# A hybrid convolution block on one core: constants on ScalarE's DMA queue, first-half squares later, the last A tile scaled by VectorE and used last in four output tiles

## The chip, the core and the metric

The kernel runs on one core of a Trainium2 chip. Five engines work side by side, each through its own instructions in order: TensorE (PE; its weight loads are listed as PEld), VectorE (DVE), ScalarE (ACT), GpSimd (POOL) and SyncE (SP). They wait for each other through semaphores. Transfers between the chip's main memory (HBM) and the on-chip memory (SBUF) are issued from the queues of SP, ACT or POOL and run on 16 DMA engines. Matmul results land in PSUM banks of 128 x 512 float32. The metric is the device time of one execution in microseconds (us); lower is better.

## The reference, cut to what matters

```python
h = rmsnorm(x, norm_mix_g)                       # x: 1024 positions x 1024 channels
z = h @ w_in                                     # 1024 -> 2560 columns
a_h, a_bg, a_cg, b_val, b_gate = split(z)        # 512 columns each
y_a = a_bg * dwconv(a_cg * a_h, conv_a_w)        # 3 taps
u = b_val * sigmoid(b_gate)
u = dwconv(u, conv_b_w) + conv_b_b               # 31 taps
y_b = silu(layernorm(u, ln_b_g, ln_b_b))
x = x + concat(y_a, y_b) @ w_out                 # 1024 -> 1024
h = rmsnorm(x, norm_ffn_g)
g = dwconv(h @ w_gate, conv_ffn_w)               # 1024 -> 2816
v = h @ w_up
x = x + (silu(g) * v) @ w_down
return rmsnorm(x, norm_final_g)
```

## The kernel before

Activations lie transposed: channels on the 128 partitions, the 1024 positions along the row, worked on as two halves h = 0 and 1 of 512. A channel tile is 128 channels, so a contraction over 1024 channels is eight steps k. To keep float32 accuracy every operand is split into a rounded part hi and a remainder lo, and each product is three matmuls: hi by hi, hi by lo, lo by hi (lines 152 to 154 are those three in the output stage, line 166 in the input projection, line 271 in its first two tiles).

**Start (lines 248 to 282).** The transfers of x go on SP's queue in pieces (line 249 on), the first two weight tiles `win01` on ACT's queue in three pieces of 2, 2 and 4 steps k (`load_w01`, `cuts`), and the constants `cst` (gains, conv taps, biases; 119 KB) on POOL's queue (line 251). For each half and each k, `load_h1` makes hi (ACT, line 213) and lo (DVE, line 214) of x times its gain, which needs `cst`; `split_w01` makes hi (a cast) and lo (a subtraction) of the weights on DVE; then six matmuls follow (three for each of the weight tiles `pg` and `pv`). `sq_h1` squares x on ACT (lines 221, 224) and adds the square to `acc1[h]` (line 226), on POOL for the whole first half and for k = 1, 2 of the second, else on DVE. `stat_h1` turns the sum into 1/rms: the sum over partitions is two matmuls with a tile of ones (`total_parts`, `total_of`, lines 179 to 186), then a root on ACT and a reciprocal on DVE (lines 193, 194). The first half's stands behind k = 3 of the second half, the second half's behind step k = 5 of the next weight tile. Since 1/rms is applied to the products, the matmuls don't wait for it, but the B tiles do.

**B tiles and conv (lines 288 to 343).** Four B tiles u are made from pairs of products; the 31-tap convolution over them is done mostly by DVE, a tap an instruction (line 315), into `cv` in PSUM and at last into `c`. It is put behind everything urgent by a priority offset.

**A tiles (lines 346 to 367).** Four tiles j: m = c times h times 1/rms squared, the three taps into y (ACT line 359, DVE lines 360 and 361), y times 1/rms (`r1`, on POOL, line 362), times b from PSUM (DVE, line 366), and the split into `yA` (hi on ACT, lo on POOL).

**Layernorm and output projection (lines 370 to 468).** `layernorm(h)` makes the four B tiles `yB[h]` from `c`: sums on DVE, totals on PE, the division (line 385), silu and hi on ACT, lo on DVE. The contraction of the output projection runs over yA tiles 0 to 3 (k = 0 to 3) and yB tiles 0 to 3 (k = 4 to 7). For the first half, the first HEAD = 4 output tiles dt are begun with the A tiles 0 to 2 (`range(NJ - 1)`) and finished, after `layernorm(0)`, with A tile 3 and the B tiles. Then come the other four tiles of the first half and eight of the second; `out_done` adds x and sums squares.

The rest is the feed-forward part (two-level products with seven instead of eight block products, line 546) and the final norm; its code isn't touched. Most of the program is put in order by a scheduler that estimates the times of instructions itself and takes `urgent` (raised priority) and `late` into account; only where a `manual_schedule` names an engine does that engine keep the written order. PE has it in the start.

Of the kernel before, what the change touches and what calls it, by code (L numbers as in the profile page):

```python
# [45 lines left out]
def block_kernel(ctx: ExitStack, tc, xT, win01, win, wout, wgate, wup, wdown, consts, outT):  # L46
# [196 lines left out]
    def split_w01(a, b):  # L243
        for i, (hi, lo) in enumerate(w01):
            nc.vector.tensor_copy(hi[:, a:b, :], raw01[:, a:b, i, :])
            minus(nc.vector, lo[:, a:b, :], raw01[:, a:b, i, :], f32(hi[:, a:b, :]))

    cuts = ((0, 2), (2, 4), (4, 8))
    nc.sync.dma_start(xs[0][:, 0, :], xT[0, :, 0])
    load_w01(*cuts[0])  # L250
    nc.gpsimd.dma_start(cst, consts)
    nc.sync.dma_start(xs[0][:, 1, :], xT[0, :, 1])
# [8 lines left out]
    with tc.manual_schedule(engines={nc.tensor.engine}):  # L261
        for h in range(2):
            for k in range(KD):
                load_h1(h, k)
                if h == 0:
                    for a, b in cuts:
                        if k == a:
                            split_w01(a, b)
                for wz, xz in ((0, 0), (0, 1), (1, 0)):
                    for pt, w in zip((pg, pv), w01):  # L270
                        nc.tensor.matmul(pt[h], w[wz][:, k, :], a1(h, k)[xz], start=k + wz + xz == 0, stop=k == KD - 1 and wz == 1)  # L271
                sq_h1(h, k)
                if h == 1 and k == 3:
                    with urgent():
                        stat_h1(0)

        def late_stat(k):
            if k == 5:
                with urgent():
                    stat_h1(1)  # L280
# [65 lines left out]
    for j in range(NJ):  # L346
# [8 lines left out]
        with urgent():  # L355
# [5 lines left out]
            nc.vector.scalar_tensor_tensor(y[:, : S - 1], m[:, 1:], col(W_A + 3 * j + 2), y[:, : S - 1], ALU.mult, ALU.add)  # L361
            pool(y, y, r1, ALU.mult)
        pb = mm_tile(base + 2, a1)
# [29 lines left out]

    def out_mm(pt, e, w, h, ks):
        for k in ks:
            mm3(half(pt, e), w[0][:, k, :], w[1][:, k, :], *y_of(h, k), k == 0, k == KD - 1)

# [44 lines left out]
    for h in range(2):  # L442
# [8 lines left out]
        for dt in range(head):  # L451
            start(dt)
            out_mm(pts[dt // 2], dt % 2, ws[dt], h, range(NJ - 1))
        if h == 0:
# [3 lines left out]
        for dt in range(KD):  # L458
            nc.sync.dma_start(half(xr[dt], h), xT[h, :, dt])
            if dt >= head:  # L460
                start(dt)
            out_mm(pts[dt // 2], dt % 2, ws[dt], h, range(NJ - 1 if dt < head else 0, KD))
            out_done(pts[dt // 2], dt, h, accs2[h])
# [683 lines left out]
```

## Time and profile before

| | |
|---|---|
| times of three runs | 1007.45, 1007.51, 1008.87 us; median 1007.51 |
| profiled execution | 1008.48 us, its span 1006.7 us |
| busy in the span | PE 967.7 us (96%), DVE 744.7 (74%), ACT 447.2 (44%), POOL 441.3 (44%) |
| chain that ended last | PE 85%, DVE 7%, issue 3%, DMA 2%, ACT 2%, POOL 1% |

The span is the profiled part of an execution. PE is busy nearly throughout, so the time is PE's work plus the places where PE stands idle or runs at the lower clock. A view of waits says what PE waited for; a timeline by engine shows the instructions of a stretch with their durations and, in brackets, the idle time ahead and who ended it. Neighbouring instructions of one form are merged (x2, x7), and a duration includes the overlap with the next instruction.

### The profile page before, as it was taken

The page shows a single profiled execution, that of the slowest core. Times are in us where ns is not written, and L with a number is a line of the kernel's source. Part 1 is how long each engine was busy: PE and PEld are TensorE (multiplying, and loading weights), DVE is VectorE, ACT ScalarE, POOL GpSimd, SP SyncE. Part 2 cuts the span into 40 slices and gives each one's busy share as a digit, 9 for nine tenths or more (in the row PEclk, how much of TensorE's full clock was granted, in tenths as well). Part 3 has the DMA queues.
Part 4 walks back from the last instruction along what each step waited for, and adds up shares of the span by engine and source line. Part 5 has one row for each costly group of instructions (what it writes and reads, how often), then busy time and mean ns, then how long its engine had stood idle before and what let it go on. Part 6 is the DMA issues. An engine that isn't in the chain of part 4 may idle for free.

```text
span 1006.7 us, 11592 instructions
## 1 busy us (share of the span) xinstructions
PE 967.7 (96%) x4208; PEld 792.3 (79%) x4208; DVE 744.7 (74%) x893; ACT 447.2 (44%) x626; POOL 441.3 (44%) x301
## 2 busy tenths in 40 slices
PE   5999999998999999899999999999999899999994
PEld 4888888886888887788888888888777688888883
DVE  7899999999679797754654554564559798796556
ACT  7354421234564446443443443443447253543353
POOL 4189853344763005454344345335324545352006
PEclk9999999999999999999999999999999999999998
DMA  6211111123564203233223232223375753643205
GB/s 255 84 43 63 42 43 63 42 63 105 177 210 129 91 1 120 100 105 132 78 105 121 89 105 108 102 94 106 109 241 172 236 163 109 195 135 101 68 0 168
DMA packets 63178, 112.56 MB, mean 112 GB/s; under 512 B 5488, under 2 KB 26992, under 8 KB 62864
## 3 DMA queue, kind: packets, MB, share of 16 engines
q1 hardware_dynamic: 62640, 110.65, 33.1%
q10 hardware_dynamic: 432, 1.05, 0.3%
q8 instruction: 33, 0.54, 0.2%
q14 instruction: 25, 0.20, 0.1%
q0 software_dynamic: 48, 0.12, 0.0%
HBM read 84.79 MB, written 27.00 MB: 111 GB/s over the span
## 4 chain that ended last, share of the span: by engine, by line
PE 85%; DVE 7%; issue 3%; DMA 2%; ACT 2%; POOL 1%; SPq 0%; POOLq 0%; DVEq 0%; ACTq 0%
PE a L546 28%; PE mm L166 19%; PE c L546 13%; PE b L546 7%; PE mm L152 3%; PE mm L154 3%; PE mm L153 3%; PE a L681 2%; PE mm L271 2%; PE c L681 1%; DVE r L93 1%; DVE wlo L93 1%; PE y L154 1%; PE y L152 1%; PE y L153 1%
## 5 line engine op out<-in xcount | busy, mean ns | idle before, releaser
L166 PE MATMUL mm<-r,whi 128*128 128x512 f32 x576 | 155.3, 389 | 0.0
L546 PE MATMUL a<-r,whi 128*128 128x512 f32 x472 | 147.4, 393 | 5.6 <-ACT a L531 4.6
L315 DVE SCALAR_TENSOR_TENSOR cv<-u,cst,cv 128x512 f32<-128x512 f32 x203 | 138.9, 748 | 0.7
L166 PEld LDWEIGHTS mm<-r,whi 128*128 128x128 f32 x576 | 108.1, 188 | 22.5
L546 PE MATMUL c<-r,whi 128*128 128x512 f32 x392 | 120.7, 389 | 0.0
L93 POOL TENSOR_TENSOR wlo<-raw,whi 128x1024 fp32r<-128x1024 f32 x30 | 76.7, 2556 | 83.0 <-ACT whi L131 83.0
L131 ACT ACTIVATE whi<-raw 128x1024 fp32r<-128x1024 f32 (+1 forms) x68 | 69.3, 1020 | 97.1 <-PE mm L166 33.0
L546 PEld LDWEIGHTS a<-r,whi 128*128 128x128 f32 x472 | 89.1, 189 | 26.4 <-ACT a L531 5.5
L500 POOL TENSOR_TENSOR s<-up 128x512 f32<-128x512 f32 (+1 forms) x31 | 43.2, 1395 | 135.5 <-DMA up<-wup 118.8
L500 POOL TENSOR_TENSOR s<-raw,s 128x512 f32<-128x512 f32 (+1 forms) x31 | 40.1, 1292 | 138.6 <-DVE wlo L93 128.7
L546 PE MATMUL a<-r,wlo 128*128 128x512 f32 x236 | 93.0, 394 | 2.3 <-DVE wlo L93 2.3
L166 PE MATMUL mm<-r,wlo 128*128 128x512 f32 x288 | 90.2, 389 | 0.0
L131 ACT ACTIVATE whi<-s 128x1024 fp32r<-128x1024 f32 (+1 forms) x52 | 52.2, 1004 | 78.2 <-POOL s L500 59.7
L546 PEld LDWEIGHTS c<-r,whi 128*128 128x128 f32 x392 | 73.6, 188 | 15.3
L93 DVE TENSOR_TENSOR wlo<-s,whi 128x1024 fp32r<-128x1024 f32 (+1 forms) x52 | 63.9, 1229 | 27.7 <-ACT whi L131 27.6
L90 POOL TENSOR_TENSOR t<-t 128x512 f32<-128x512 f32 x36 | 53.8, 1506 | 65.3 <-DVE t L603 65.3
L624 DVE TENSOR_TENSOR t<-a,c 128x512 f32<-128x512 f32 x40 | 27.4, 686 | 68.1 <-issue 37.3
L546 PE MATMUL c<-r,wlo 128*128 128x512 f32 x196 | 76.3, 389 | 0.0
L531 ACT ACTIVATE a<-a 128x512 f32<-128x512 f32 x76 | 45.1, 593 | 64.0 <-PE a L546 61.3
L546 PE MATMUL a<-r,ahi 128*128 128x512 f32 x224 | 70.5, 396 | 1.0 <-DVE xd L862 1.0
L546 PE MATMUL b<-r,whi 128*128 128x512 f32 x232 | 71.4, 389 | 0.0
L131 ACT ACTIVATE r<-r 128x512 fp32r<-128x512 f32 x71 | 43.8, 628 | 52.9 <-DMA r<-ydT 25.6
(213 smaller groups left out, 2111.2 us busy)
## 6 DMA issues: line engine op xcount, KB each, us to landing
raw<-wgate SPq DMA_DIRECT2D x22, 512.0 KB, 4.7
up<-wup SPq DMA_DIRECT2D x20, 512.0 KB, 3.4
raw<-win SPq DMA_DIRECT2D x18, 512.0 KB, 3.2
ydT<-t SPq DMA_DIRECT2D x36, 256.0 KB, 2.0
r<-ydT SPq DMA_DIRECT2D x36, 256.0 KB, 3.4
raw<-wout SPq DMA_DIRECT2D x16, 512.0 KB, 3.6
ydB<-t SPq DMA_DIRECT2D x27, 256.0 KB, 2.0
r<-ydB SPq DMA_DIRECT2D x27, 256.0 KB, 4.5
```

What stands on the lines that cost most here:

```text
L90: nc.gpsimd.tensor_tensor(out=out, in0=a, in1=b, op=op)
L93: eng.tensor_tensor(out=out, in0=a, in1=b, op=ALU.subtract)
L131: nc.scalar.activation(hi, y, AF.Copy)
L152: nc.tensor.matmul(out, whi, hi, start=first, stop=False)
L153: nc.tensor.matmul(out, whi, lo, start=False, stop=False)
L154: nc.tensor.matmul(out, wlo, hi, start=False, stop=last)
L166: nc.tensor.matmul(outs[h], w, a[h][z], start=s0, stop=s1)
L315: nc.vector.scalar_tensor_tensor(fin if k == KC - 1 else acc, src, w, acc, ALU.mult, ALU.add)
L500: self.eng.tensor_tensor(out=self.t[:, i * self.w : (i + 1) * self.w], in0=a, in1=b, op=op)
L531: nc.scalar.activation(t, b, AF.Copy)
L546: nc.tensor.matmul(out, w[wz][:, k, :], x[xz], start=first and k + wz + xz == 0, stop=k == n - 1 and wz == 1, skip_group_check=not first)
L681: nc.tensor.matmul(out, w[wz][:, k, :], xz, start=first and k == 0 and wz == 0 and xz is hi, stop=not first and k == 3 and wz == 1)
```

## The change

It has three parts. (1) The constants go first on ACT's DMA queue, ahead of the three pieces of `win01`, and no longer on POOL's. (2) The hi parts of the third piece of the weights (k = 4 to 7) are made by ACT instead of DVE; the squares of the first half are written later: k = 0 to 3 beside steps 4 to 7 of the first half, k = 4 to 7 beside steps 0 to 3 of the second; the first half's 1/rms stands behind k = 7 of the second half, the second half's behind step k = 6 of the next tile. (3) For the last A tile, y times 1/rms is done by DVE; and the first four output tiles take the four B tiles first and A tile 3 last.

```diff
@@ split_w01, transfers
-            nc.vector.tensor_copy(hi[:, a:b, :], raw01[:, a:b, i, :])
+            if a < 4:
+                nc.vector.tensor_copy(hi[:, a:b, :], raw01[:, a:b, i, :])
+            else:
+                nc.scalar.activation(hi[:, a:b, :], raw01[:, a:b, i, :], AF.Copy)
...
     nc.sync.dma_start(xs[0][:, 0, :], xT[0, :, 0])
+    nc.scalar.dma_start(cst, consts)
     load_w01(*cuts[0])
-    nc.gpsimd.dma_start(cst, consts)
...
-                sq_h1(h, k)
-                if h == 1 and k == 3:
+                if h == 0 and k >= 4:
+                    sq_h1(0, k - 4)
+                if h == 1:
+                    if k < 4:
+                        sq_h1(0, k + 4)
+                    sq_h1(1, k)
+                if h == 1 and k == 7:
                     with urgent():
                         stat_h1(0)
...
-            if k == 5:
+            if k == 6:
                 with urgent():
                     stat_h1(1)
...
-            pool(y, y, r1, ALU.mult)
+            if j == NJ - 1:
+                nc.vector.tensor_tensor(out=y, in0=y, in1=r1, op=ALU.mult)
+            else:
+                pool(y, y, r1, ALU.mult)
...
-    def out_mm(pt, e, w, h, ks):
+    def out_mm(pt, e, w, h, ks, last=True):
         for k in ks:
-            mm3(half(pt, e), w[0][:, k, :], w[1][:, k, :], *y_of(h, k), k == 0, k == KD - 1)
+            mm3(half(pt, e), w[0][:, k, :], w[1][:, k, :], *y_of(h, k), k == 0, last and k == ks[-1])
...
-            out_mm(pts[dt // 2], dt % 2, ws[dt], h, range(NJ - 1))
+            out_mm(pts[dt // 2], dt % 2, ws[dt], h, range(NJ - 1), False)
...
-            out_mm(pts[dt // 2], dt % 2, ws[dt], h, range(NJ - 1 if dt < head else 0, KD))
+            out_mm(pts[dt // 2], dt % 2, ws[dt], h, [*range(NJ, KD), NJ - 1] if dt < head else range(KD))
```

Where this moves instructions is the scheduler's doing, and is seen in the built programs. ACT in the start, from its first hi part of x on, before (r_94 is hi of the first half, r_96 of the second; c and u hold x of the first and second half):

```order
L213 ACTIVATE r_94<-c,cst 128x512 [waits DMASW0_49]
L213 ACTIVATE r_94<-c,cst 128x512 [waits DMAHW2_49]
L224 ACTIVATE sq<-c 128x512
L213 ACTIVATE r_94<-c,cst 128x512 [waits DMAHW4_49]
L224 ACTIVATE sq<-c 128x512
L213 ACTIVATE r_94<-c,cst 128x512
L224 ACTIVATE sq<-c 128x512
L213 ACTIVATE r_94<-c,cst 128x512 [waits DMAHW6_49]
```

and after, from the third hi part on, to the hi parts of the second half (whi_120 and whi_122 are the two weight tiles, k = 4 to 7):

```order
L213 ACTIVATE r_94<-c,cst 128x512 [waits DMAHW4_49]
L213 ACTIVATE r_94<-c,cst 128x512
L224 ACTIVATE sq<-c 128x512 x2
L213 ACTIVATE r_94<-c,cst 128x512 [waits DMAHW6_49]
L213 ACTIVATE r_94<-c,cst 128x512
L224 ACTIVATE sq<-c 128x512 x2
L248 ACTIVATE whi_120<-rr 128x512 [waits DMAHW7_49]
L248 ACTIVATE whi_122<-rr 128x512
L213 ACTIVATE r_94<-c,cst 128x512 [waits DMAHW0_49]
L213 ACTIVATE r_94<-c,cst 128x512
```

On ACT two casts of weights stand now between the squares and the hi parts of k = 6 and 7, and six squares of the first half (the first stands behind the hi part of k = 1) lie ahead of them; the squares of k = 6 and 7 stand further back, among those of the second half.

DVE from the last A tile's taps to its product with b, before (m3 and y3 are the last A tile, r0_94 takes the lo parts of the B tiles, cv_1018 is the conv):

```order
L360 SCALAR_TENSOR_TENSOR y3_1662<-m3_1661,cst_90,y3_1662 128x1023 [waits Activation_49]
L315 SCALAR_TENSOR_TENSOR cv_1018<-u_100,cst_90,cv_1018 128x512 [waits DVE_49]
L93 TENSOR_TENSOR r0_94<-c_101,r0_94 128x512 [waits PE_49,Activation_49]
L361 SCALAR_TENSOR_TENSOR y3_1662<-m3_1661,cst_90,y3_1662 128x1023 [waits DVE_49]
L93 TENSOR_TENSOR r0_94<-c_101,r0_94 128x512 [waits PE_49,Activation_49]
L315 SCALAR_TENSOR_TENSOR cv_1018<-u_100,cst_90,cv_1018 128x512 [waits DVE_49]
L93 TENSOR_TENSOR r0_94<-c_101,r0_94 128x512 [waits PE_49,Activation_49] x2
L315 SCALAR_TENSOR_TENSOR cv_1018<-u_100,cst_90,cv_1018 128x512 [waits DVE_49]
L366 TENSOR_TENSOR y3_1662<-mm_1734,y3_1662 128x512 [waits Pool_49]
L366 TENSOR_TENSOR y3_1662<-mm_1735,y3_1662 128x512 [waits PE_49]
```

and after, from its second tap on:

```order
L369 SCALAR_TENSOR_TENSOR y3_1662<-m3_1661,cst_90,y3_1662 128x1023 [waits DVE_49]
L93 TENSOR_TENSOR r0_94<-c_101,r0_94 128x512 [waits PE_49,Activation_49]
L323 SCALAR_TENSOR_TENSOR cv_1018<-u_100,cst_90,cv_1018 128x512 [waits DVE_49]
L93 TENSOR_TENSOR r0_94<-c_101,r0_94 128x512 [waits PE_49,Activation_49]
L371 TENSOR_TENSOR y3_1662<-y3_1662,rr_102 128x1024 [waits DVE_49]
L93 TENSOR_TENSOR r0_94<-c_101,r0_94 128x512 [waits PE_49,Activation_49]
L323 SCALAR_TENSOR_TENSOR cv_1018<-u_100,cst_90,cv_1018 128x512 [waits DVE_49]
L93 TENSOR_TENSOR r0_94<-c_101,r0_94 128x512 [waits PE_49,Activation_49]
L377 TENSOR_TENSOR y3_1662<-mm_1734,y3_1662 128x512 [waits DVE_49]
L377 TENSOR_TENSOR y3_1662<-mm_1735,y3_1662 128x512 [waits PE_49]
```

The product y3 times rr (1/rms) is DVE's now, between the lo parts of the second and the third B tile.

PE behind the first 29 matmuls of the four head tiles (mm_1801, 1802, 1827, 1828), which stand the same in both, before (r4_98 is yA of the first half, r0_94 its yB):

```order
L152 MATMUL mm_1801<-r4_98,whi_1667 128x512 [waits Activation_49]
L152 MATMUL mm_1802<-r4_98,whi_1730 128x512
L152 MATMUL mm_1827<-r4_98,whi_1823 128x512
L154 MATMUL mm_1828<-r4_98,wlo_1841 128x512 [waits Pool_49]
L152 MATMUL mm_1828<-r4_98,whi_1840 128x512
```

and after:

```order
L152 MATMUL mm_1801<-r0_94,whi_1667 128x512
L152 MATMUL mm_1802<-r0_94,whi_1730 128x512
L153 MATMUL mm_1801<-r0_94,whi_1667 128x512 [waits DVE_49]
L154 MATMUL mm_1801<-r0_94,wlo_1668 128x512
L152 MATMUL mm_1801<-r0_94,whi_1667 128x512 [waits Activation_49]
L153 MATMUL mm_1802<-r0_94,whi_1730 128x512
L154 MATMUL mm_1802<-r0_94,wlo_1731 128x512
L152 MATMUL mm_1802<-r0_94,whi_1730 128x512
L154 MATMUL mm_1828<-r4_98,wlo_1841 128x512 [waits Pool_49]
```

The wait for hi of A tile 3 that stood there is 28 matmuls further back; in its place PE waits for the lo part of the first B tile. In the second half, the second total of `layernorm(1)` stands 17 matmuls further back in PE's order than before. Behind the output projection the engines' orders are the same.

## Rows read from the trace of the kernel before

**Rows 1.** The page, share of each engine in the chain of work that ended last.

```profile
PE 85%; DVE 7%; issue 3%; DMA 2%; ACT 2%; POOL 1%; SPq 0%; POOLq 0%; DVEq 0%; ACTq 0%
```

**Rows 2.** The waits of PE over the whole span: who was waited for, us in total, times, the longest.

```profile
PE mm L271 <- DVE r L214: 5.7, 3, 2.9
...
PE mm L152 <- ACT r L131: 3.5, 1, 3.5
PE mm L271 <- ACT r L213: 3.1, 1, 3.1
```

**Rows 3.** Busy time by stretch: us, then busy us and instructions of PE, PEld, DVE, ACT and POOL, granted PE clock, DMA share, GB/s.

```profile
100.00:200.00 100.00, 100.00 (x442) 82.82 (x442) 95.13 (x141) 28.64 (x37) 54.56 (x31) 1.00 0.14 48
200.00:250.00 50.00, 46.52 (x199) 37.94 (x198) 49.54 (x61) 19.92 (x27) 23.05 (x11) 0.97 0.27 85
```

**Rows 4.** Timeline of PE in the start (start, us, instruction, in brackets the idle time ahead and its releaser); the row without an engine's operation is of the chain of waits (start, us, what), further on.

```profile
8.21 2.08 PE L271 MATMUL mm<-r,whi 128*128 128x512 f32 x4 [3.13 <-ACT r L213]
...
19.13 0.72 PE L271 MATMUL mm<-r,whi 128*128 128x512 f32 x2 [2.88 <-DVE r L214]
...
22.10 0.73 PE L271 MATMUL mm<-r,whi 128*128 128x512 f32 x2 [1.31 <-DVE r L214]
...
38.75 8.17 PE mm L166 x36
...
46.76 0.39 PE L185 MATMUL total<-st,ones_r 128*128 128x512 f32 x1
```

**Rows 5.** Timeline of ACT in the start.

```profile
7.43 1.34 ACT L213 ACTIVATE r<-c,cst 128x512 fp32r<-128x512 f32 x2 [1.81 <-DMA cst<-consts]
...
9.67 0.72 ACT L213 ACTIVATE r<-c,cst 128x512 fp32r<-128x512 f32 x1 [0.38 <-DMA c<-xT]
...
10.30 0.61 ACT L224 ACTIVATE sq<-c 128x512 f32<-128x512 f32 x1
...
10.82 0.71 ACT L213 ACTIVATE r<-c,cst 128x512 fp32r<-128x512 f32 x1
...
11.43 0.62 ACT L224 ACTIVATE sq<-c 128x512 f32<-128x512 f32 x1
```

**Rows 6.** Timelines of DVE and of POOL (the adds of squares, and one product of the same size alone) in the start.

```profile
9.37 10.85 POOL L226 TENSOR_TENSOR acc<-acc,sq 128x512 f32<-128x512 f32 x7 [7.29 <-ACT sq L224]
9.92 2.95 DVE L93 TENSOR_TENSOR wlo<-rr,whi 128x256 fp32r<-128x256 f32 x2
...
12.79 1.75 DVE L214 SCALAR_TENSOR_TENSOR r<-c,cst,r 128x512 fp32r<-128x512 f32 x1
...
21.30 2.73 DVE L214 SCALAR_TENSOR_TENSOR r<-c,cst,r 128x512 fp32r<-128x512 f32 x4
...
29.28 0.68 DVE L93 TENSOR_TENSOR st<-acc,st 128x512 fp32r<-128x512 f32 x1
...
32.54 2.34 DVE L93 TENSOR_TENSOR wlo<-raw,whi 128x1024 fp32r<-128x1024 f32 x2
...
48.20 3.35 DVE L194 RECIPROCAL rr<-std 128x512 f32<-128x512 f32 x1 [2.42 <-ACT std L193]
...
53.81 1.04 POOL L90 TENSOR_TENSOR rr<-rr 128x512 f32<-128x512 f32 x1
```

**Rows 7.** Transfers issued in the first microseconds: queue, count, KB each, us from issue to landing. The first is that of the weights that was issued first on ACT's queue.

```profile
rr<-win ACTq DMA_DIRECT2D x1, 256.0 KB, 4.4
...
cst<-consts POOLq DMA_DIRECT2D x1, 119.0 KB, 6.2
```

**Rows 8.** Timeline of PE at the head tiles of the output projection.

```profile
242.25 0.39 PE L153 MATMUL mm<-r,whi 128*128 128x512 f32 x1
246.12 1.05 PE L152 MATMUL mm<-r,whi 128*128 128x512 f32 x3 [3.48 <-ACT r L131]
...
249.96 0.54 PE L152 MATMUL mm<-r,whi 128*128 128x512 f32 x1
250.33 0.39 PE L153 MATMUL mm<-r,whi 128*128 128x512 f32 x1
```

**Rows 9.** Timeline of DVE ahead of it.

```profile
231.82 2.48 DVE L385 TENSOR_TENSOR c<-c,u 128x512 f32<-128x512 f32 x4
234.22 1.28 DVE L360 SCALAR_TENSOR_TENSOR y<-m,cst,y 128x1023 f32<-128x1023 f32 x1
235.42 0.75 DVE L315 SCALAR_TENSOR_TENSOR cv<-u,cst,cv 128x512 f32<-128x512 f32 x1
...
239.13 5.01 DVE L93 TENSOR_TENSOR r<-c,r 128x512 fp32r<-128x512 f32 x2
...
244.73 1.27 DVE L366 TENSOR_TENSOR y<-mm,y 128x512 f32<-128x512 f32 x2
```

**Rows 10.** Timelines of ACT and POOL at the same place.

```profile
245.44 1.23 ACT L131 ACTIVATE r<-y 128x512 fp32r<-128x512 f32 x2 [6.79 <-DVE y L366]
238.10 2.71 POOL L90 TENSOR_TENSOR y<-y,rr 128x1024 f32<-128x1024 f32 x1 [7.92 <-DVE y L361]
240.78 2.81 POOL L93 TENSOR_TENSOR wlo<-raw,whi 128x1024 fp32r<-128x1024 f32 x1
```

**Rows 11.** The second layernorm: PE's second total of it, the last lo part of its B tiles on DVE, and PE's matmuls about that time.

```profile
273.34 0.40 PE L186 MATMUL total<-st,ones_r 128*128 128x512 f32 x1
288.62 2.29 DVE L93 TENSOR_TENSOR r<-c,r 128x512 fp32r<-128x512 f32 x1
...
291.71 0.61 PE L153 MATMUL mm<-r,whi 128*128 128x512 f32 x2
```

## The prediction

> **What bounds the kernel now.** I read the chain of work first: 85% of it is PE [rows 1]. So the time is PE's own work, which the change leaves alone (as many matmuls before as after), plus what PE loses in waits and at the lower clock. The view of PE's waits names the places: 8.8 us for hi and lo parts of x (ACT line 213, DVE line 214), which are the first two tiles, and one wait of 3.5 us for ACT's split at line 152, which is the first output tile [rows 2]. The change touches just these two. The third view to read is the table by stretch: between them PE has nothing to wait for, but DVE is 95% busy from 100 to 200 us and 99% from 200 to 250 [rows 3]. A gain of PE must therefore be asked at every step whether DVE follows.
>
> **Part 1, the constants.** In the profile ACT's first hi part waits for them until 7.43, and PE's first real matmul stands behind it at 8.21 [rows 4, 5]. They took 6.2 us on POOL's queue; a transfer of twice the size, first on ACT's queue, took 4.4 [rows 7]. From there I put their landing at 5.2 at the latest and the first matmuls some 2 us earlier. The weights queue one place later, about 0.5 us, which DVE has to spare at 8.9. By itself all this brings nothing: PE stops again at 19.13 and 22.10 for lo parts [rows 4], and a stretch ahead of a later wait is lost. It is costed at nothing; its cover is part 2.
>
> **Part 2, the start.** What ends last is the wait at 22.10, for the lo part of k = 4. By then PE has done the 24 matmuls of k = 0 to 3 and two of k = 4; behind it there is none to the end of the stage. From there a matmul takes 8.17 / 36 = 0.227 us [rows 4]. The cause is DVE: from 9.37 to 20.2 POOL adds seven squares without a pause, 1.55 us each, and in that time every DVE instruction of two inputs takes 1.5 to 1.75 us, against 0.68 later (2.73 / 4), whether it is 256 or 512 wide; a POOL product of that size takes 1.04 alone [rows 6]. The two alternate, one waits for the other.
>
> After the change the last thing to come for k = 4 is the second lo part of the weights. ACT sets its earliest time: from 9.67, when the third piece of x lands, four hi parts at 0.61 and four squares and two casts at 0.52 (I price the casts as squares, of the same width) make 5.6 us [rows 5], so 15.2; two subtractions of 0.68 [rows 6] end at 16.6. That is the best bound. The worst is DVE in step with POOL all the way: from the third hi part, 10.4, six instructions (four lo parts, two subtractions) of 1.75 end at 20.9. I take the case between: six at 0.68 and four adds of 1.04 that come in between (the squares now reach POOL in pairs, as ACT gets to them), 10.4 + 4.1 + 4.2 = 18.7. PE has then done 29 matmuls, which in the profile it has at 22.10 + 3 x 0.227 = 22.8. **Gain 4.1 us, between 1.9 and 6.2.**
>
> A wait is added. The first half's total now stands behind all 96 matmuls and needs the sum of squares, whose lo part is a DVE instruction behind ten lo parts, four adds and two wide subtractions. PE comes there at 18.7 + 67 x 0.227 + 0.2 = 34.1. DVE needs for these, the lo part itself included, 15 x 0.68 + 2.34 = 12.5 us [rows 6], so it is there at 31.2, or with four adds of POOL in the way at 35.4. Queued behind it on PE is the next weight tile. **Cost 0 to 1.3 us; I take 0.7**, the middle, since about half of the adds fall into DVE's own waits. Start: 3.4 us.
>
> DVE itself starts its conv stage with the second half's reciprocal, at 48.20, which follows PE's total at 46.76 [rows 4, 6]. After, that total stands at 34.8 + 0.5 + 42 x 0.227 = 44.8: DVE moves forward by 2.0 us, PE by 3.4. So DVE lies 1.4 us nearer to PE than before; over the saturated stretch it has little idle time to make that up.
>
> **Part 3, the output tiles.** PE goes from the matmul at 242.25 to that at 250.33, twelve further in its order, in 8.1 us; at 0.227 these are 2.7. **5.4 us** are lost: 3.5 idle, and the rest because ten matmuls behind the wait, 246.12 to 249.96, take 0.38 on the mean instead of 0.227, at the lower clock level: the granted clock of 200 to 250 is 0.97, that of the stretch before 1.00 [rows 3, 8]. The wait is for A tile 3: POOL's product from 238.10, DVE's two products with b at 244.73 behind two subtractions that took 5.0 us beside POOL, ACT's split at 245.44 [rows 9, 10].
>
> After, PE needs at that point the first B tile's lo part, two matmuls on, at 242.9 on the old scale, 241.5 with the lag. DVE has it after four divisions to 234.3, two taps of 1.28, one of 0.75 and 0.68, at 238.3; or, if it waits for one POOL instruction (the lo part of the fourth tile's weights, 2.8), at 241.1. No wait. Then come on DVE a tap, three subtractions, a tap and the product with 1/rms, which I price by the tap of nearly the same width, 1.28: another 4.8 us, 245.9 at the worst, against 22 matmuls on, 247.5 minus 1.4. A tile 3 follows at 247.7, wanted 28 on, at 247.4. So 0 to 0.3 us are left of a wait of 3.5, no idle time long enough to lower the clock, and the 5.4 come back whole.
>
> Here one rule speaks against the change. The two subtractions of 5.0 us show that a DVE instruction of two SBUF inputs waits out a POOL instruction [rows 9, 10]. The Trainium skill, SBUF — State Buffer, section Who interferes with whom, says so of every such instruction, so also of the product that is moved to DVE. By that rule, should a further POOL subtraction of 2.8 us fall on the product, A tile 3 would come 2.8 us later and the sum would be 5.7 us instead of 8.5. I don't take it: POOL's next instruction there waits for this very product, so the only one in flight is already counted.
>
> **What is late next.** The second layernorm. In the profile its second total on PE is at 273.34 and its last lo part ends at 290.91, 17.6 us later; PE uses it about 291.7 [rows 11]. After, that total stands 17 matmuls further back, and from it to the last lo part's first use PE has 79 matmuls, 17.9 us. So 0.3 us to spare; one more subtraction held as that at 288.62 (2.29 for 0.68) would cost 1.6. **Cost 0 to 1.6; I take 0.3.** Behind it the orders are the same, and all that follows hangs on PE.
>
> **Sum.** 3.4 + 5.4 - 0.3 = 8.5 us. The profiled execution took 1008.48, 1.8 of it outside the span of 1006.7, and lies 1.0 above the median of the three runs; made against it the sum gives 1000.0, against the median 999.0, which I give. Ends: 6.2 + 5.4 = 11.6 gained, 995.9; 1.9 - 1.3 + 5.4 - 0.3 - 1.6 = 4.1 gained, 1003.4.
>
> **Rivals.** (a) The second layernorm takes the gain. Its last lo part comes when DVE gets to it, at 290.9 as before, since DVE is nearly full to 250 [rows 3] and gets the product on top. PE would want it at 242.5 - 3.4 + 208 x 0.227 = 286.3 and waits 4.6: gain 4.2, **1003.3**. Against it: the layernorm's totals are placed in PE's order and DVE's stage starts 2 us earlier. (b) The start brings nothing, because ACT, with two casts more in a row that is already full, or DVE in step with POOL, gives k = 4 no sooner: gain 5.4, **1002.1**. Against it: ACT's bound of 15.2 is far from 22. (c) The other side: DVE becomes the bound. The start brings nothing, the second total stands six matmuls later (1.4 us), the product adds 1.3 and one more POOL instruction is waited out (2.8): DVE is 5.5 us late, its last lo part comes at 296.4. In the profile PE is at that matmul at 250.33 + 197 x 0.227 = 295.1 [rows 8]; so from 4.2 us of delay the kernel is slower. The price here is 1.3 and some 1.6 for the clock behind a long wait, **1010.4**. It needs three things at once. (d) The start lost, and the layernorm late by the 1.4 and 1.3 alone: its last lo part comes at 293.6, PE wants it at 242.5 + 208 x 0.227 = 289.7 and waits 3.9: gain 1.5, **1006.0**.
>
> **How the numbers follow.** Forecast 0.62, (a) 0.12, (b) 0.13, (c) 0.07, (d) 0.06. The range takes the ends of the sum and reaches over (a) and (b): 995.9 to 1003.6. A measurement of this kernel tells about 0.2%, 2 us: faster by more 0.87, within 0.06, slower 0.07.
>
> **What would show it.** PE's last wait of the start ends near 18.7 and is for a lo part of the weights (line 93), not of x; POOL's adds of squares come with gaps, and DVE's lo parts between them take 0.7; ACT's casts end near 15.2. A wait of PE of under 1.5 us at the total about 34. The second reciprocal starts about 46. At the head tiles no wait over 0.5 us and a clock of 1.00 through. If PE instead waits at the first tiles of the second half (lines 152, 153, for DVE line 93), it is (a); if its last wait of the start still ends beyond 21, (b). The forecast is wrong as a whole if PE's waits between 50 and 230 are no longer none: then DVE, not PE, carries that stretch.

## The result, and the profile after

| | kernel before | changed kernel |
|---|---|---|
| runs, us | 1007.45 to 1012.11, median 1008.87 (5) | 1001.19 to 1003.51, median 1002.82 (5) |
| ratio | | 0.9929, 95% interval 0.9911 to 0.9946 |
| profiled execution, us | 1008.48 | 1003.51 |
| its span, us | 1006.7 | 1001.7 |

The change makes the kernel faster: by the ratio 0.71%, 7.2 us of 1008.87 (5.4 to 9.0), by the two medians 6.0 us. The forecast of 999.0 us was 8.5 less than the median of 1007.51 that was known then; measured is 1002.82. The two spans differ by 5.0 only: the profiled execution of before lies below the median of its runs, that of after is the slowest of its five. The profiles therefore tell where time went, and the ratio how much.

**The start, after.** First PE's timeline (with one of its weight loads, PEld), then DVE's and POOL's; they answer to [rows 4, 6].

```profile
6.97 0.70 PE L274 MATMUL mm<-r,whi 128*128 128x512 f32 x2 [1.53 <-DVE whi L246]
...
18.61 1.11 PE L274 MATMUL mm<-r,wlo 128*128 128x512 f32 x2 [0.53 <-DVE wlo L93]
...
19.21 0.19 PEld L274 LDWEIGHTS mm<-r,wlo 128*128 128x128 f32 x1 [0.42 <-DVE wlo L93]
...
19.56 1.10 PE L274 MATMUL mm<-r,whi 128*128 128x512 f32 x4
...
35.61 0.50 PE L186 MATMUL total<-st,ones_r 128*128 128x512 f32 x1 [0.62 <-DVE st L93]
```

```profile
6.53 0.49 DVE L246 CAST whi<-rr 128x256 fp32r<-128x256 f32 x2 [4.93 <-DMA rr<-win]
...
12.15 5.81 DVE L214 SCALAR_TENSOR_TENSOR r<-c,cst,r 128x512 fp32r<-128x512 f32 x4
17.88 1.28 DVE L93 TENSOR_TENSOR wlo<-rr,whi 128x512 fp32r<-128x512 f32 x2
...
46.85 3.35 DVE L194 RECIPROCAL rr<-std 128x512 f32<-128x512 f32 x1 [2.27 <-ACT std L193]
...
10.36 6.38 POOL L226 TENSOR_TENSOR acc<-acc,sq 128x512 f32<-128x512 f32 x4 [0.85 <-ACT sq L224]
21.26 0.11 POOL L307 MEMSET u<- 128x16 f32 x1 [4.52 <-ACT sq L224]
```

PE's last wait ends at 18.61 and is for a lo part of the weights, as forecast; it is that of the first of the two tiles, for the 29th matmul. The 30th needs the lo part of the second tile: its weight load starts at 19.21. Four adds of POOL still stretch four lo parts to 1.45 us each; from about 17 POOL is idle, and the two subtractions of the weights take 0.64 each. The first total costs a wait of 0.62.

**The head of the output tiles, after**, in PE's and DVE's timelines and by stretch [rows 3, 8, 9].

```profile
242.33 0.39 PE L154 MATMUL mm<-r,wlo 128*128 128x512 f32 x1
...
236.21 2.24 DVE L93 TENSOR_TENSOR r<-c,r 128x512 fp32r<-128x512 f32 x1
238.37 1.21 DVE L371 TENSOR_TENSOR y<-y,rr 128x1024 f32<-128x1024 f32 x1
```

```profile
200.00:250.00 50.00, 50.00 (x222) 41.34 (x221) 49.48 (x63) 21.60 (x30) 22.24 (x11) 1.00 0.26 85
```

The twelfth matmul after the place of the old wait starts at 242.33 instead of 250.33. There is no wait, and the granted clock is 1.00 instead of 0.97.

**Behind it, after**: PE, ACT and DVE at the second layernorm [rows 11]; then SP's queue, ACT, DVE and PE up to the second half's 1/rms total; then the issue at 265.01 of the weights that ACT casts at 269.54, with the us to its landing.

```profile
269.15 0.40 PE L186 MATMUL total<-st,ones_r 128*128 128x512 f32 x1
...
269.54 1.06 ACT L131 ACTIVATE whi<-raw 128x1024 fp32r<-128x1024 f32 x1 [2.93 <-PE total L186]
...
271.14 1.28 ACT L193 ACT_TABLE_LOAD   x1
272.43 0.69 ACT L193 ACTIVATE u<-total,eps_l 128x512 f32<-128x512 f32 x1
...
273.15 3.35 DVE L194 RECIPROCAL u<-u 128x512 f32<-128x512 f32 x1 [3.97 <-ACT u L193]
...
284.51 4.17 DVE L93 TENSOR_TENSOR r<-c,r 128x512 fp32r<-128x512 f32 x2 [1.48 <-ACT r L131]
...
287.03 0.50 PE L153 MATMUL mm<-r,whi 128*128 128x512 f32 x1 [0.94 <-DVE r L93]
...
288.73 0.50 PE L153 MATMUL mm<-r,whi 128*128 128x512 f32 x1 [0.27 <-DVE r L93]
```

```profile
288.70 0.33 SPq L470 DMA_DIRECT2D c<-xT  x1
289.12 0.38 SPq L127 DMA_DIRECT2D raw<-wout  x1
...
294.43 1.06 ACT L131 ACTIVATE whi<-raw 128x1024 fp32r<-128x1024 f32 x1 [3.58 <-DMA raw<-wout]
...
297.32 0.69 ACT L193 ACTIVATE std<-total,eps_r 128x512 f32<-128x512 f32 x1
...
298.44 3.34 DVE L194 RECIPROCAL rr<-std 128x512 f32<-128x512 f32 x1
...
332.07 0.50 PE L185 MATMUL total<-st,ones_r 128*128 128x512 f32 x1 [0.17 <-ACT st L179]
...
332.80 0.50 PE L186 MATMUL total<-st,ones_r 128*128 128x512 f32 x1 [0.22 <-DVE st L93]
```

```profile
raw<-wout SPq DMA_DIRECT2D x1, 512.0 KB, 4.4
```

The same two places in the kernel before, ACT and DVE at the layernorm, then SP's queue and DVE:

```profile
272.22 1.28 ACT L193 ACT_TABLE_LOAD   x1
...
274.49 3.35 DVE L194 RECIPROCAL u<-u 128x512 f32<-128x512 f32 x1 [2.96 <-ACT u L193]
...
291.36 0.38 SPq L127 DMA_DIRECT2D raw<-wout  x1
...
300.68 3.34 DVE L194 RECIPROCAL rr<-std 128x512 f32<-128x512 f32 x1
```

Here part of the gain goes again. Before, DVE's reciprocal began 1.15 us after the second layernorm's total (273.34, 274.49); after, 4.0 later (269.15, 273.15). Behind the total there now stand on ACT a cast of output weights, a square, a load of activation tables (1.28 us) and only then the square root; before, the table load was over (at 273.50) when the total came. The cast starts 0.1 us after its weights landed (269.43). The profile puts its wait down to PE's total, which ends at 269.54 too; but with this cast on DVE (further on) it starts at 269.17, before that total begins (269.20), and there the profile names the transfer. So ACT waited for the weights. They had been issued 0.4 us behind a store on SP's queue, and that store behind a residual add of DVE that ended at 264.55. PE stops twice for lo parts. Later SP's queue holds output weights behind loads of x that overwrite what the layernorm's last lo part (until 288.68) reads; ACT's next square root stands behind the cast of these weights, and DVE's work up to the last total behind that.

To compare kernels I follow five places of PE's order, in us earlier (-) than in the profile of before, counted in PE's timeline: the first matmul of the output projection, its 60th, the first of the feed-forward stage, the second half's 1/rms total, and the end of the span. Each ratio is against runs of the kernel before taken beside it.

| kernel | head | 60th | feed-forward | 1/rms total | span | ratio (95%) |
|---|---|---|---|---|---|---|
| before, at | 235.91 | 254.68 | 329.83 | 338.31 | 1006.7 | |
| changed | -2.7 | -8.0 | -6.3 | -5.5 | -5.0 | 0.9929 (0.9911 to 0.9946) |
| changed again | -2.1 | -7.5 | -5.6 | -4.7 | -5.6 | 0.9924 (0.9911 to 0.9938) |
| start only | -2.7 | -3.2 | -3.2 | -3.3 | -2.9 | 0.9964 (0.9951 to 0.9978) |
| head only | -0.1 | -5.5 | -4.8 | -4.7 | -4.6 | 0.9959 (0.9947 to 0.9971) |
| without reordering | -2.9 | -6.3 | -4.9 | -4.6 | -5.6 | 0.9932 (0.9920 to 0.9943) |
| product on POOL | -2.3 | -7.7 | -4.4 | -4.2 | -4.7 | 0.9941 (0.9929 to 0.9953) |
| constants back | -1.7 | -7.1 | -5.4 | -4.7 | -4.7 | 0.9945 (0.9927 to 0.9963) |
| casts back | -1.6 | -7.0 | -5.4 | -4.6 | -5.4 | 0.9938 (0.9922 to 0.9954) |
| squares back | -1.7 | -7.1 | -6.3 | -5.5 | -6.1 | 0.9932 (0.9914 to 0.9949) |
| longer head, half 2 | -2.8 | -8.2 | -7.5 | -5.9 | -6.2 | 0.9924 (0.9909 to 0.9939) |
| casts to DVE | -2.6 | -8.0 | -5.8 | -3.3 | -3.8 | 0.9956 (0.9938 to 0.9973) |
| both of these | -2.6 | -8.0 | -6.8 | -3.9 | -5.1 | 0.9953 (0.9936 to 0.9970) |
| longer head, x by ACT | -2.8 | -8.2 | -7.6 | -7.4 | -6.2 | 0.9917 (0.9897 to 0.9936) |

From the last total to the end the fourteen profiles take between 667.2 and 669.5 us, before 668.4; so a span tells nothing below some 2 us.

### The profile page after: what moved, and what is told of

It is laid out like the page before. It is cut to its first block, busy times and chain, and to the rows that moved or that the text cites. A ratio compares the mean times of both kernels' runs of the same rounds, so it can differ in the third digit from the quotient of the medians.

```text
span 1001.7 us, 11591 instructions
## 1 busy us (share of the span) xinstructions
PE 968.2 (97%) x4208; PEld 790.8 (79%) x4208; DVE 739.2 (74%) x892; ACT 448.5 (45%) x628; POOL 438.5 (44%) x299
## 4 chain that ended last, share of the span: by engine, by line
PE 78%; DVE 9%; ACT 4%; DMA 3%; issue 3%; POOL 1%; SPq 0%; POOLq 0%; DVEq 0%; ACTq 0%
PE a L557 29%; PE mm L166 20%; PE c L557 13%; PE b L557 7%; DVE r L93 2%; PE c L692 1%; PE a L692 1%; PE mm L153 1%; PE mm L152 1%; PE mm L154 1%; PE y L154 1%; PE y L152 1%; PE y L153 1%; DVE wlo L93 1%; DMA c<-xT 1%
```

## Experiments

Each diff is against the changed kernel unless it says otherwise.

### Each part alone

**Start only** (parts 1 and 2).

```diff
-            if j == NJ - 1:
-                nc.vector.tensor_tensor(out=y, in0=y, in1=r1, op=ALU.mult)
-            else:
-                pool(y, y, r1, ALU.mult)
+            pool(y, y, r1, ALU.mult)
...
-            out_mm(..., [*range(NJ, KD), NJ - 1] if dt < head else range(KD))
+            out_mm(..., range(NJ - 1 if dt < head else 0, KD))
```

> Parts 1 and 2 alone, the output tiles as before. PE reaches the head of the output tiles 2.65 us early, as in the profile of the changed kernel, but DVE only 1.35 (its second reciprocal started at 46.85 instead of 48.20). Theory (what the start earns passes the head only as far as DVE moved): the wait for A tile 3 grows from 3.5 to about 4.8 us, behind it PE is 1.35 early, and it stays so: about 1.3 us less in the profile. Rival (PE sets it, the forecast's own start): 2.65 to 3.4 us less. Second rival: nothing, the wait takes all.

The theory fell; the rival's amount holds, by another way than it named: 3.2 us behind the head, a ratio of 0.9964 (3.6 us, 2.2 to 4.9). PE's timeline at the head of this kernel:

```profile
244.43 1.62 PE L152 MATMUL mm<-r,whi 128*128 128x512 f32 x4 [2.91 <-ACT r L131]
```

Before, the wait stood ahead of the 30th matmul of the output projection and ended at 246.12 [rows 8]; here it stands ahead of the 37th. A tile 3 came 1.7 us sooner, and the scheduler had put seven more matmuls (1.6 us at 0.227) ahead of it: 3.3. An edit at 10 us changed the order at 240.

**Head only** (part 3), the diff of parts 1 and 2 undone:

```diff
-    nc.scalar.dma_start(cst, consts)
     load_w01(*cuts[0])
+    nc.gpsimd.dma_start(cst, consts)
...
-                nc.scalar.activation(hi[:, a:b, :], raw01[:, a:b, i, :], AF.Copy)
+            nc.vector.tensor_copy(hi[:, a:b, :], raw01[:, a:b, i, :])
...
-                if h == 1 and k == 7:
+                sq_h1(h, k)
+                if h == 1 and k == 3:
...
-            if k == 6:
+            if k == 5:
```

> Part 3 alone, the start as before. 5.4 us are recovered at the head. Theory (the second layernorm's chain stands on DVE's pace, which is then 1.35 us later while PE is 2.65 later): PE's wait for the layernorm's lo parts is 0.4 us, not 1.75, some 0.7 more go at the 1/rms total: about 4.3 us less in the profile. Rival (the chain from the second total is anchored on PE, since ACT's square root stands behind a cast of weights that waits for PE to free a buffer, so that PE finds it as late wherever it starts): a wait of 1.75 again, 3.0 us less. By the forecast, nothing late: 5.4 less.

5.4 us come back at the head, as forecast; 0.7 is gone at the feed-forward stage, 0.8 at the total. That is nearest to the theory's 4.3, though nearly all of the loss is at the layernorm and 0.1 at the total, where 0.7 was expected. Start and head alone, 0.9964 and 0.9959, multiply to 0.9923, and both together measured 0.9929: in time they add up within the intervals.

**Without the reordering** (the product of A tile 3 stays on DVE), and **with the product on POOL** (the reordering stays). The diffs are the second and the first piece of that of the start alone.

> The changed kernel without the reordering: only the product of A tile 3 on DVE is left of part 3. From the profile of the changed kernel A tile 3's first hi part is there at 242.6 instead of 245.9, PE wants it at 239.7: theory, a wait of 2.9 us at the head and some lower clock behind it, 3.3 us less than the kernel before, none lost later, since PE then comes later to the layernorm. Rival (the product alone does it): as the changed kernel, 5 us less in the profile.

> The changed kernel with the product of A tile 3 left on POOL: only the reordering of part 3. PE wants A tile 3 at about 244.2; the lo parts on POOL ended there at 244.1 to 245.3. Theory (the reordering is what counts, POOL's product comes at most 1.5 us later than DVE's): a wait of 0 to 1.4 us in the head, some of which the later wait at the layernorm takes up, 4 to 5 us less than the kernel before. Rival (both parts are needed): a wait of 2.8 us or more, 2.2 us less or worse.

The first theory was too hard on the lone half, the second holds. Without the reordering PE waits 1.2 us, not 2.9:

```profile
242.53 1.20 PE L152 MATMUL mm<-r,whi 128*128 128x512 f32 x4 [1.19 <-ACT r L131]
```

The order again had 36 matmuls ahead of it. With the product on POOL there is no wait at the head, though DVE's two subtractions are held for 5.04 us as before [rows 9]; the first B tile fills the time. So either half does most of part 3: 6.3 or 7.7 of 8.0 us at the 60th matmul, and 4.6, 4.2 and 5.5 at the last total. What the second half adds at the head is mostly lost behind it, and the ratios (0.9932, 0.9941, 0.9929) can't be told apart.

### Each edit of the start undone

```diff
-    nc.scalar.dma_start(cst, consts)
     load_w01(*cuts[0])
+    nc.gpsimd.dma_start(cst, consts)
```

> The changed kernel with part 1 undone: the constants on POOL's queue again. Forecast's theory (by itself part 1 brings nothing, PE stops again for lo parts): the first matmul is back at 8.2, PE's last wait of the start still ends within 0.5 of 18.6, and the time is that of the changed kernel within 0.5 us. Rival (all of ACT's and DVE's chain of the start begins with the constants): the last wait ends 1.2 to 2.5 us later, and as much is lost.

```diff
-                if h == 0 and k >= 4:
-                    sq_h1(0, k - 4)
-                if h == 1:
-                    if k < 4:
-                        sq_h1(0, k + 4)
-                    sq_h1(1, k)
-                if h == 1 and k == 7:
+                sq_h1(h, k)
+                if h == 1 and k == 3:
...
-            if k == 6:
+            if k == 5:
```

> The changed kernel with the squares of the first half again beside its lo parts, and the two totals where they were; the casts stay on ACT and the constants on its queue. Forecast's theory (POOL's adds, in step with DVE's instructions of two inputs, make the start late): lo parts of 1.5 to 1.75 us again, the last wait ends at 21 or later, 2.5 to 3.5 us of the start are lost, no wait at the first total, and the time is 4 us under the kernel before, as with part 3 alone. Rival (the casts off DVE were what counts): the last wait ends before 19.5 and the time stays that of the changed kernel.

```diff
-            if a < 4:
-                nc.vector.tensor_copy(hi[:, a:b, :], raw01[:, a:b, i, :])
-            else:
-                nc.scalar.activation(hi[:, a:b, :], raw01[:, a:b, i, :], AF.Copy)
+            nc.vector.tensor_copy(hi[:, a:b, :], raw01[:, a:b, i, :])
```

> The changed kernel with the casts of the weights' second half back on DVE; constants and squares stay as changed. At the head of the output tiles PE was 2.65 us early in the changed kernel, 1.7 with the constants back and 1.7 with the squares back. Theory (the three edits of the start add up): the casts are worth the rest, 0.8, so PE is 1.8 us early here, and the time is within 1 us of that of the changed kernel, since the second layernorm takes up what comes early. Rival (the casts carry the start: with them on DVE the weights' lo parts wait for DVE as before): the last wait ends beyond 20.5, PE is less than 1 us early at the head.

In nine profiles with the start as changed the head begins at 233.02 to 233.81, 233.3 on the mean; seven lie within 0.3 us, and the two late ones, the changed kernel again (233.81) and that with the product on POOL (233.65), ran part of the start at the lower clock (a granted clock of 0.57 from 19 to 23 us in the one, with its row in the last section, and from 16 to 20 us in the other, where the changed kernel's first profile has 1.00). Undone it begins at 234.19 (constants), 234.31 (casts) and 234.21 (squares): 0.9, 1.0 and 0.9 us later, one profile each, and these three make 2.8 where 2.6 were gained. So the edits add up, and none carries the start. Part 1, costed at nothing, is worth a third of it: without it the last wait of the start ends at 19.45, not 18.61 (for a lo part of x), and the 31st matmul is 0.9 later. With the casts on DVE the last wait ends at 17.98 and the 31st matmul is where it was (19.52 and 19.56), but DVE is late further on: PE waits 0.31 at 29.98 and 1.12 at the first total. With the squares back the last wait ends at 20.43 and lo parts take 1.72 us beside POOL, but no wait is left at the first total, so 1.8 us at the one place are 0.9 at the head. PE's last wait, then POOL and DVE of that kernel:

```profile
20.43 1.11 PE L274 MATMUL mm<-r,wlo 128*128 128x512 f32 x2 [1.56 <-DVE wlo L93]
...
9.73 9.49 POOL L226 TENSOR_TENSOR acc<-acc,sq 128x512 f32<-128x512 f32 x6 [1.21 <-ACT sq L224]
...
14.61 5.16 DVE L214 SCALAR_TENSOR_TENSOR r<-c,cst,r 128x512 fp32r<-128x512 f32 x3
```

In time none of the three can be told from the changed kernel, and with the squares back PE is as early at the last total as with them moved (5.5). The theory of 2.5 to 3.5 us for the squares and that of nothing for the constants fell; that the edits add up holds.

### Where the gain goes behind the head

**The changed kernel again**, beside the next three on one chip.

> The changed kernel once more, to stand beside the next three on one chip: 0.993 of the kernel before (between 0.991 and 0.995), 5 to 7 us less; in the trace the same two losses behind the head, about 1.7 us at the second layernorm and 0.7 at the second 1/rms total.

It repeats: 0.9924; of 7.5 us behind the head 1.9 are gone at the feed-forward stage and 1.0 more at the last total.

**A longer head in the second half**:

```diff
-        head = HEAD if h == 0 else 0
+        head = HEAD if h == 0 else 3
...
-            out_mm(pts[dt // 2], dt % 2, ws[dt], h, range(NJ - 1), False)
+            out_mm(pts[dt // 2], dt % 2, ws[dt], h, range(NJ - 1 if h == 0 else NJ), False)
...
-            out_mm(..., [*range(NJ, KD), NJ - 1] if dt < head else range(KD))
+            out_mm(..., ([*range(NJ, KD), NJ - 1] if h == 0 else range(NJ, KD)) if dt < head else range(KD))
```

> The changed kernel, and the second half too begins three output tiles with A tiles alone: 12 more matmuls (2.7 us) stand ahead of the first B tile's lo part. Theory 1 (the second layernorm stops PE only because PE runs out of other work): its waits of 1.2 and 0.4 us go, PE is at the feed-forward 7.8 instead of 6.25 us early, and most of it stays: 1.5 us less than the changed kernel. Theory 2 (ACT and DVE, whose chain from the second layernorm to the second 1/rms total is late, set the end of the stage): what PE gains it gives back at that total, the wait there grows from 0.7 to about 2, and the time is that of the changed kernel.

```profile
PE total L185 <- ACT st L179: 1.0, 1, 1.0
...
PE total L186 <- DVE st L93: 0.9, 2, 0.7
...
PE mm L153 <- DVE r L93: 0.4, 1, 0.4
```

In its waits of PE the layernorm costs 0.4 instead of 1.2 to 1.3, and PE is 7.5 us early at the feed-forward stage; at the total it waits about 1.2 (0.99 and 0.22), and 1.6 of the 7.5 are gone. The time is that of the changed kernel (1002.04 and 1002.19): theory 2. So the layernorm's stop is real, and by itself worth little, because another chain ends just behind it.

**The two casts ahead of the square roots put on DVE**, alone and with the longer head:

```diff
-        split(raw, hi, lo, nc.gpsimd if idx >= 6 else nc.vector)
+        if idx in (29, 33):
+            nc.vector.tensor_copy(hi, raw)
+            minus(nc.gpsimd, lo, raw, f32(hi))
+        else:
+            split(raw, hi, lo, nc.gpsimd if idx >= 6 else nc.vector)
```

> The changed kernel with the two casts of weights that stand ahead of square roots on ACT (269.54 to 270.6 and 294.43 to 295.5) put on DVE. In the profile of the changed kernel the second layernorm's total ended at 269.6 and the square root began at 272.43; the first half's 1/rms total ended at 292.2 and its root began at 297.32. Theory 2: the root of the layernorm comes 1 to 2.4 us sooner, the other one 2 us or more, PE's waits for the lo parts and for the second 1/rms total go: 1.5 to 2.4 us less than the changed kernel. Rival (DVE stands behind the same freed buffer and the same transfer as ACT did): the reciprocals start where they did, 273.1 and 298.4, no change.

> Both of these edits together. Theory 1: as with the longer head alone, 1.5 us less than the changed kernel. Theory 2: as with the casts alone or up to 0.5 better, 1.5 to 2.9 us less. If neither edit does anything alone and both do it together, each had hidden the other's wait.

DVE of the first, at both places:

```profile
269.17 1.18 DVE L140 CAST whi<-raw 128x1024 fp32r<-128x1024 f32 x1 [0.53 <-DMA raw<-wout]
...
273.65 3.35 DVE L198 RECIPROCAL u<-u 128x512 f32<-128x512 f32 x1 [2.70 <-ACT u L197]
...
294.91 0.69 DVE L140 CAST whi<-raw 128x1024 fp32r<-128x1024 f32 x1 [4.22 <-DMA raw<-wout]
...
298.90 3.35 DVE L198 RECIPROCAL rr<-std 128x512 f32<-128x512 f32 x1 [0.22 <-ACT std L197]
```

The rival holds, and worse: the reciprocals start at 273.65 and 298.90, the residual adds now stand behind the casts on DVE, and ACT's squares of them are what its roots wait for. The total is 1.4 us later than in the changed kernel beside it, the time 3.0. So at the second place it is not the cast that holds the chain but the transfer ahead of it. At the first the theory fell with nothing gained: DVE's reciprocal follows the layernorm's total by 4.0 us with the cast on ACT and by 4.4 with it on DVE (269.20, 273.65), against 1.15 in before and with the start alone. The cast itself starts 0.4 us sooner, but ACT's square now waits for the residual add behind it on DVE, and the table load and the root stand behind the square. With both edits PE is 6.8 us early at the feed-forward stage, 3.9 at the total, and the time is 1004.95: neither theory's 1.5 us came.

**That transfer moved off SP's queue**, on top of the longer head:

```diff
-            nc.sync.dma_start(half(xr[dt], h), xT[h, :, dt])
+            q = nc.scalar if h == 1 and 2 <= dt < 6 else nc.sync
+            q.dma_start(half(xr[dt], h), xT[h, :, dt])
```

> The run with the longer head in the second half, and the second half's x for output tiles 2 to 5 loaded by ACT's queue instead of SP's. In the profile of the changed kernel SP's queue stood on these loads until 288.70 (they overwrite what the second layernorm's last lo part, to 288.68, reads); the output weights queued behind them were issued at 289.12 and landed at 294.43, ACT's cast of them and behind it the square root of the first half's 1/rms (297.32) waited, and DVE's reciprocal began at 298.44. Before, the same chain lay 2.2 us later (290.94, 291.36, 300.68). Theory 2, made precise (the second layernorm's last lo part sets, through SP's queue, when ACT and DVE get to the second 1/rms total): the weights are issued 2 us sooner, the reciprocal begins at 295 to 297, the wait at the second total goes, and PE keeps the 7.5 us that it had at the feed-forward: 1.5 to 2 us less than the changed kernel. Rival (DVE's own work to that total sets it): the reciprocal comes sooner, the wait at the total stays 1.5 us or more, and the time is that of the changed kernel.

SP's queue, ACT and DVE of this kernel:

```profile
286.25 0.33 SPq L127 DMA_DIRECT2D raw<-wout  x1
...
291.84 1.07 ACT L131 ACTIVATE whi<-raw 128x1024 fp32r<-128x1024 f32 x1 [0.34 <-PE mm L153]
...
294.75 0.69 ACT L193 ACTIVATE std<-total,eps_r 128x512 f32<-128x512 f32 x1
...
295.86 3.34 DVE L194 RECIPROCAL rr<-std 128x512 f32<-128x512 f32 x1
```

The weights are issued 2.9 us sooner than in the changed kernel, the cast no longer waits for a transfer, the reciprocal starts at 295.86 instead of 298.44, there is no wait at the last total, and PE keeps 7.4 of its 7.6 us to that place. The mechanism is shown: the longer head without this edit kept 5.9. The gain in time is not: 0.9917 (0.9897 to 0.9936) beats the kernel before, but can't be told from 0.9929 and 0.9924, and its profile gave 1.2 us back between that total and the end.

## Why the prediction was right, by its steps

The time lies in the range, the side is right, and 8.5 us is inside what the ratio allows (5.4 to 9.0). But the median of 1002.82 is only 0.8 inside the range's upper end, and nearer to rivals (b), 1002.1, and (a), 1003.3, than to 999.0; the time alone does not choose between them, the trace does. In it 5.5 of the 8.5 stand at the last total: the start gave 2.65 for 3.4, the head 5.4 as forecast, the second layernorm took 1.8 for 0.3, and the last total took 0.7 for nothing. The place and size of the head's gain were foreseen; that the time still lies in the range, with three misses all to one side, is owed to the range's width.

- **Part 1** (costed at nothing, cover in part 2): the step failed in kind. The constants landed by 4.65 (5.2 at the latest), the first matmul moved by 1.24 us, not 2, since the weights' first piece behind them came 1.35 later (6.53 for 5.18), not 0.5, a price for which no row stood. But undoing it costs 0.9 at the head: an edit early in a chain of alternating engines is not lost at the next wait if it is that chain which ends the wait.
- **Part 2**: the wait ended where forecast (18.61 and 18.7), ACT's casts sooner (14.3 and 15.2). But 18.7 was forecast for the second lo part, and that let the 30th matmul start at 19.22: 3.7 us early against 22.90 in before, instead of 4.1. Behind the first total, with a wait of 0.6 (0.7 forecast), 2.65 were left where 3.4 were forecast. The inner story was half right: POOL's four adds fell on the lo parts of x, and the subtractions found POOL idle. DVE's second reciprocal moved by 1.35, not 2.0.
- **Part 3** (5.4 lost, all come back): 5.4 in the changed kernel and 5.4 alone, from the head to the 60th matmul. That the product isn't held by POOL holds too: it took 1.21 us from 238.37, with POOL idle from 237.90 to 242.79. One subtraction was held, 2.24, until just behind POOL's (237.90). The Trainium skill, SBUF — State Buffer, section Who interferes with whom, is borne out by that subtraction, and the second stall that it would have allowed didn't come. Not seen: that either half of part 3 does nearly all.
- **Second layernorm** (17.6 us of chain against 17.9 of matmuls, 0.3): mis-sized. The wait named as rival (a), for DVE line 93, came in small: 1.8 us (1.9 in the repeat) from the 60th matmul to the feed-forward stage, just beyond the bound of 1.6, where (a) had 4.6. The chain was taken from before as a fixed length; with the total 17 matmuls further back it was 19.5 long (269.15 to 288.68). The reciprocal came 2.85 us later behind the total than before, because the cast, the square and the table load stood ahead of the root; the rest of the chain was 0.9 shorter (15.5 for 16.4), although a POOL subtraction (to 286.42) and the add behind it held the last two lo parts (4.17 us, where two take 1.36).
- **"Behind it the orders are the same, and all that follows hangs on PE"**: this step failed. DVE's reciprocal for the first half moved by only 2.24 us, as much as the layernorm's last lo part (290.91 to 288.68), through SP's queue and ACT (before, ACT's cast there started 0.6 us behind the landing, put down to PE); 0.7 to 1.0 us were lost at the last total. The run with x on ACT's queue shows it.
- **Rivals (b) to (d)** did not come: PE's last wait of the start ended at 18.61, not beyond 21; PE waits nowhere between 36 and 286; and the layernorm's last lo part came at 288.68, not at 293.6 or 296.4.

With part 3 in, the reciprocal stands 3.3 to 6.6 us behind the layernorm's total, and the traces show on what that hangs in nine of those twelve kernels: in each, ACT's cast starts 0.1 us behind the landing of its weights, the reciprocal comes 3.2 us behind the landing (3.7 with a square between), and the weights are issued 0.4 us behind another issue of SP's queue. No run moves that issue, so what the wait there is worth in time stays open, as does whether the 2.3 us of spread behind the last total are chance.

## What to carry to other kernels

A gain on the bounding engine is kept only as far as the next chain that runs over other engines moves as well; take such a chain's length from the order after the change, not from the trace before, and follow every in-order queue on it (ACT's casts and table loads ahead of a root, loads and stores on SP ahead of weights), because what a queue's head waits for holds all behind it. When two halves of an edit each remove most of a wait, test them apart. And moving a cast to the engine that waits for its result can only move the queue, as it did here.

## What the runs showed of the hardware that had not been expected

A load of activation tables took 1.28 us on ACT ahead of the layernorm's square root, in both kernels. Before, it ran while the root still waited for the total (272.22 to 273.50); after, it stood between the total and the root (271.14 to 272.43).

A transfer of 119 KB put first on ACT's queue landed 3.9 us after issue, against 6.2 on POOL's [rows 7], and the 256 KB behind it on the same queue landed 1.35 us later than before. The issue rows of the changed kernel:

```profile
rr<-win ACTq DMA_DIRECT2D x2, 256.0 KB, 6.3
...
cst<-consts ACTq DMA_DIRECT2D x1, 119.0 KB, 3.9
```

The clock behind a wait of PE: the stretch from 246 to 250 us had a granted clock of 0.61, a mean over the two levels of 1.2 and 2.4 GHz, behind 3.48 us idle (to 246.12), 0.70 behind 2.91 us (to 244.43), and 1.00 behind 1.19 us (to 242.53, without the reordering). The rows by stretch of before, of the start alone and of the kernel without the reordering:

```profile
246.00:250.00 4.00, 3.88 (x11) 3.02 (x12) 3.82 (x6) 0.67 (x2) 2.52 (x2) 0.61 0.41 157
```

```profile
246.00:250.00 4.00, 4.00 (x14) 3.20 (x14) 2.82 (x4) 0.00 (x0) 0.98 (x1) 0.70 0.00 0
```

```profile
246.00:250.00 4.00, 4.00 (x20) 3.29 (x19) 3.54 (x5) 1.59 (x2) 1.66 (x1) 1.00 0.17 66
```

How long PE stood idle does not settle it: behind 2.88 us in the start of before (to 19.13) the clock stayed at 1.00, and behind 1.56 us in the changed kernel again (to 18.50) it was 0.57 in the same stretch, where the first profile of the same kernel had 1.00. The rows of before and of the changed kernel again:

```profile
19.00:23.00 4.00, 2.56 (x10) 1.82 (x11) 4.00 (x6) 4.00 (x8) 1.23 (x1) 1.00 0.01 3
```

```profile
19.00:23.00 4.00, 3.90 (x10) 3.08 (x11) 4.00 (x6) 4.00 (x8) 1.86 (x3) 0.57 0.05 19
```
